# A hybrid decoder block on one core: zero matmuls before the first transposes, scale's first piece summed by TensorE, and pool means taken before the shift is added

## The chip, the cores and the metric

The kernel runs on one core of a Trainium2 chip. The metric is the device time of one execution in microseconds (us). The kernel before has a median of 923.67 us over 3 runs (922.73 to 924.28).

## The reference

One decoder block over 1024 tokens of width 1024, in float32. Two RMS norms with adaLN stand ahead of a mixer and an MLP. What matters here is the mixer's first part:

```
mod = silu(c) @ w_ada + b_ada                  # shift1, scale1, gate1, shift2, scale2, gate2
h = rms_norm(x, norm1_pre) * (1 + scale1) + shift1
z = h @ w_in                                   # 512 columns u, 512 columns v, 512 columns for the pool
v = layer_norm(gelu(v)); y_a = gelu(u) * (w_causal[head] @ v + b_spatial)      # chunks of 128 tokens
diff = mean over the last w tokens of z_b - z_b      # w = 2, 4, 8, 16 by group; at the start over the tokens there are
y_b = (diff @ w_pool[group] + b_pool) * pool_scale
mix = concat(y_a, y_b) @ w_out
```

The shift enters z as a constant row, shift1 @ w_in, the same for each token. A mean over a window less the token does not change when the same constant is added to all tokens.

## The kernel before, in words

The 1024 tokens are worked in two halves of 512. Features lie on the 128 partitions in eight blocks k, tokens along the free dimension. Every large product is made of three float32r matmuls (high by high, high by low, low by high); the high part of an operand is a ScalarE cast, the low part a VectorE subtraction.

`start()` (line 1339) is the first half's way from x to the mixer's outputs. Its instructions stand in the order written, on VectorE, ScalarE, TensorE, GpSimd and SyncE alike (`manual_schedule`, line 1664). What follows, `project()` among it, is ordered by the planner: it takes what is ready by its own costs, and may put such instructions between those of `start()`. In `start()`:

1. *Norm and transposes.* `first(i)` squares token tile i on ScalarE and has GpSimd take the power, `second(i)` scales the tile on VectorE, `third(i)` transposes three feature blocks on TensorE. `vectors_a()` transposes the loaded vectors.
2. *Scale in pieces.* `piece()` loads columns of w_ada, `piece_sum()` (line 1306) weighs eight tiles with silu(c) on VectorE into two accumulators and adds them (`both`), `piece_end()` (line 1322) sums over partitions by a matmul with ones, and `ada_vector()` (line 183) makes scale or shift of it. PIECES (line 1289) are 128, 128, 256, 256 and 256 columns.
3. *Pool.* `scaled_hi`, `scaled_lo` write a block's scaled tokens, and `pool_pass(k, n)` (line 1417) multiplies them with the pool columns of w_in, into four PSUM banks `pbs`. The shift is not in it yet.
4. *Values.* A loop over four pairs of blocks (line 1552) makes v with `value_step`, and beside it the shift's pieces. `row_sum` (line 1522) builds shift @ w_in for the three parts on VectorE, in `vacc`, `bacc` and `uacc`, and `row_vector` (line 1528) sums it over partitions on TensorE.
5. *Gates.* `gate_pass(k)` (line 1591) makes u; `values()` (line 442) is the layer norm of v. Then `row_vector(bacc)` gives the pool's shift, four ScalarE activations add it to the four zb tiles (line 1634), and `windowed(h, j, zb)` (line 379) keeps the last 16 tokens for the second half (halo), widens the window in one to four steps, corrects the first tokens and subtracts. `pool_out` multiplies with w_pool, `spatial_products` and `spatial_end` make the gated part.
6. *Output.* `stream.fill(n)` (line 28) makes sure that n tiles of w_out are loaded, cast and subtracted; `load_x(1)` loads the second half's tokens, into the buffers in which the pool columns of w_in lay (`braw`, line 1348); `normalise(1)` scales them. `project(0)` (line 554) multiplies with w_out, pool outputs first (MIX_ORDER), in two output halves, with the transposes of the second tokens between.

Buffers: tag `raw` has four, which hold one shift accumulator, the four u pairs `uraw` and then the w_out tiles; tags `whi`, `wlo` have four each, tag `acc` four, PSUM eight banks. The program prints the code:

Of the kernel before, what the change touches and what calls it, by code (L numbers as in the profile page):

```python
# [8 lines left out]
F32 = mybir.dt.float32  # L9
# [7 lines left out]
P = 128  # L17
# [23 lines left out]
def block_kernel(  # L41
# [78 lines left out]
    make_identity(nc, ident)  # L120
    ones = const.tile([P, P], F32, name="ones")
# [1184 lines left out]
    def piece_sum(blk, c0, n, ts):  # L1306
# [9 lines left out]
        def both():  # L1316
            a, b = [acc_of[blk][o][:, c0:c0 + n] for o in range(2)]
            nc.vector.tensor_tensor(a, a, b, ALU.add)

        return [step(kt) for kt in range(KT)] + [both]  # L1320

    def piece_end(blk, c0, n, split=False):
        pa = ps_tile(f"pa{blk}_{c0}")
        nk = n // P
        for k in range(nk):
            at = c0 + k * P
            nc.tensor.matmul(pa[:, k:k + 1], lhsT=acc_of[blk][0][:, at:at + P], rhs=ones[:, 0:1], start=True, stop=True)
        rest = lambda: ada_vector(blk, pa[:, 0:nk], range(c0 // P, c0 // P + nk))
        return rest if split else rest()
# [9 lines left out]
    def start():  # L1339
# [44 lines left out]
        def second(i):  # L1384
            nc.vector.tensor_scalar(xs[i], xs[i], rs[i], None, ALU.mult)
# [5 lines left out]
        g = piece_sum(1, *PIECES[0], sc[0])  # L1391
        first(0)
        first(1)
        vectors_a()
        second(0)
# [3 lines left out]
        third(1)  # L1399
        first(3)  # L1400
        second(2)
        third(2)
        weave(g)
        second(3)
        scale_rest = piece_end(1, *PIECES[0], split=True)
        third(3)
        scale_rest()
# [7 lines left out]
        pbs = [ps_tile(f"pb0_{j}") for j in range(NG)]  # L1415
# [23 lines left out]
        pool_pass(0, 0)  # L1439
        pool_pass(0, 1)  # L1440
        piece_end(1, *PIECES[1])
# [64 lines left out]
        value_lo(0, 1)  # L1506
        pool_pass(KT - 1, 1)
# [12 lines left out]
        bacc, vacc, uacc = rows_of("b"), rows_of("v"), accp.tile([P, 512], F32, tag="junk", bufs=1, name="shift_wu")  # L1520
# [31 lines left out]
        for kp in range(NQ):  # L1552
            if kp == 0:
                sh.append(piece(0, 2 * QC, QC))
                value_tiles(1)
                value_hi(1)
# [25 lines left out]
            if kp == 1:  # L1582
                rest_b()
                turn()
            if kp == 2:
                offsets()

# [28 lines left out]
        weave(sums_b(0, 4), sums_u(0, 2))  # L1616
        gate_load(3)
        gate_pass(2)
        gate_pass(3)
        steps, vs = values(0, pvs)  # L1620
        weave(steps[:4], sums_b(4, 8))
# [4 lines left out]
        weave(steps[4:], sums_u(2, 6))  # L1626
        gate_hi(3)
        gate_lo(3, 0)
        gate_lo(3, 1)
        gate_pass(5)  # L1630
        bvec = row_vector(bacc, "b")
        for j in range(NG):
            z = zbs[j][:, HALO:]
            nc.scalar.activation(z, z, AF.Identity, bias=bvec[:, j:j + 1])
        weave(sums_u(6, 8), windowed(0, 0, zbs[0]))
        gate_pass(6)
        gate_pass(7)
        psp = [spatial_products(0, j, vs) for j in range(2)]
        uvec = row_vector(uacc, "u")
        us = [gate(0, j, pus[j], uvec[:, j:j + 1]) for j in range(NHEAD)]  # L1640
        weave(windowed(0, 1, zbs[1]), windowed(0, 2, zbs[2]))
        psp += [spatial_products(0, j, vs) for j in range(2, NHEAD)]
        yb = [pool_out(0, j, pair_of(diffs[0], j)) for j in range(2)]
        weave(windowed(0, 3, zbs[3]))
# [3 lines left out]
        yb += [pool_out(0, j, pair_of(diffs[0], j)) for j in range(2, NG)]  # L1648
        load_x(1)
        measure, apply = normalise(1, "a")  # L1650
        ya = []
        for j in range(NHEAD):
            if j in (1, 2):
                stream.fill(1 + j)
            ya.append(spatial_end(0, j, psp[j], us[j]))
            if j < 2:
                yb[2 + j][1]()
            if j == 2:
                measure()
# [50 lines left out]
```

## Time and profile before

| | |
|---|---|
| median of 3 runs | 923.67 us (922.73 to 924.28) |
| the profiled execution | 922.04 us |
| its span, first to last instruction | 920.3 us |
| TensorE busy (matmul) | 889.4 us, 97% of the span |
| VectorE busy | 687.4 us, 75% |
| ScalarE busy | 419.1 us, 46% |
| GpSimd busy | 89.1 us, 10% |
| chain that ended last, by engine | TensorE 53%, issue 32%, VectorE 8%, ScalarE 4%, DMA 2% |

Busy time is a union over instructions of an engine; matmuls are pipelined, so that a row of x8 matmuls shows the time from the first start to the last end. A timeline row has the start, the time, the engine, the source line and what was written and read; a bracket behind it gives the idle time before, and what ended it. One fp32 matmul has two records.

### The profile page before, as it was taken

Reading aid. Unit: us, or ns where it says so; the run is one execution under the profiler, and the core shown is the slowest. Engines: PE = TensorE matmul, PEld = TensorE weight load, DVE = VectorE, ACT = ScalarE, POOL = GpSimd, SP = SyncE. Lnnn points to the kernel's source line nnn. Section 1 sums busy time; section 2 is a strip of 40 time slices with the busy share of each in tenths; the row PEclk is TensorE's granted clock in tenths of the full one; section 3 lists DMA queues with packets and bytes.
Section 4 is the critical chain, followed back from the end, with each engine's and each line's share of the span. In section 5 each row is a group of like instructions: output and inputs, shape, how many; then the busy total and the mean of one; then the engine's idle time right before and its main releaser. Section 6 shows DMA issues by size and latency. Waiting matters only on the chain.

```text
span 920.3 us, 10782 instructions
## 1 busy us (share of the span) xinstructions
PE 889.4 (97%) x3960; PEld 722.9 (79%) x3960; DVE 687.4 (75%) x980; ACT 419.1 (46%) x558; POOL 89.1 (10%) x147
## 2 busy tenths in 40 slices
PE   5999999999999989999999999999999999999995
PEld 3788678888887768888888888778888888888883
DVE  6989888799759896766666657567887774569796
ACT  3323674334367474444444354544455433434331
POOL 4001020013003001111100101100000000000032
PEclk9999999999999999999999999999999999999998
DMA  9934256575734148543444434499975884334664
GB/s 316 357 113 143 91 161 188 178 252 183 234 87 149 54 129 274 185 138 130 168 150 158 139 136 155 160 320 389 338 242 198 294 279 117 109 110 145 207 212 154
DMA packets 114105, 173.52 MB, mean 189 GB/s; under 512 B 6098, under 2 KB 61442, under 8 KB 114052
## 3 DMA queue, kind: packets, MB, share of 16 engines
q1 hardware_dynamic: 104292, 135.03, 45.8%
q0 software_dynamic: 9760, 37.80, 10.8%
q8 instruction: 31, 0.51, 0.2%
q14 instruction: 22, 0.18, 0.1%
HBM read 135.06 MB, written 37.75 MB: 188 GB/s over the span
## 4 chain that ended last, share of the span: by engine, by line
PE 53%; issue 32%; DVE 8%; ACT 4%; DMA 2%; POOL 1%; SPq 0%; POOLq 0%; DVEq 0%; ACTq 0%
PE a L828 6%; PE a L829 6%; PE a L830 6%; PE p L830 3%; PE p L829 3%; PE p L828 3%; PE pb L1421 3%; PE po L85 2%; PE pu L1596 2%; PE po L86 2%; PE po L87 2%; PE pv L85 2%; PE pv L87 2%; PE pv L86 2%; PE b L828 1%
## 5 line engine op out<-in xcount | busy, mean ns | idle before, releaser
L85 PE MATMUL m<-thi,shi 128*128 128x512 f32 x448 | 174.3, 389 | 0.0
L86 PE MATMUL m<-tlo,shi 128*128 128x512 f32 x448 | 174.3, 389 | 0.0
L87 PE MATMUL m<-thi,slo 128*128 128x512 f32 x448 | 174.3, 389 | 0.0
L94 DVE TENSOR_TENSOR slo<-s,shi 128x1024 fp32r<-128x1024 f32 x56 | 68.4, 1222 | 55.8 <-ACT shi L91 55.8
L91 ACT CAST shi<-s 128x1024 fp32r<-128x1024 f32 x56 | 58.9, 1052 | 106.2 <-PE m L86 64.1
L86 PEld LDWEIGHTS m<-tlo,shi 128*128 128x128 f32 x448 | 84.1, 188 | 17.6
L87 PEld LDWEIGHTS m<-thi,slo 128*128 128x128 f32 x448 | 84.1, 188 | 17.5
L85 PEld LDWEIGHTS m<-thi,shi 128*128 128x128 f32 x448 | 84.1, 188 | 17.3
L91 ACT CAST thi<-wt 128x1024 fp32r<-128x1024 f32 x40 | 42.1, 1052 | 39.7 <-DVE wt L571 31.3
L91 ACT CAST whi<-w_raw 128x1024 fp32r<-128x1024 f32 x28 | 29.3, 1053 | 52.0 <-DMA w_raw<-in_w_in_dram 15.4
L571 DVE TENSOR_TENSOR wt<-wt,b 128x1024 f32<-128x1024 f32 x32 | 39.1, 1222 | 15.0 <-DMA b<-in_w_fc_dram 13.1
L94 DVE TENSOR_TENSOR tlo<-wt,thi 128x1024 fp32r<-128x1024 f32 x40 | 48.9, 1223 | 1.4
L571 DVE TENSOR_TENSOR S<-c,F 128x1024 f32<-128x1024 f32 x12 | 14.7, 1224 | 41.8 <-ACT F L860 41.8
L94 DVE TENSOR_TENSOR wlo<-w_raw,whi 128x1024 fp32r<-128x1024 f32 x28 | 34.1, 1220 | 7.0 <-ACT whi L91 7.0
L858 ACT COPY F<-a 128x512 f32<-128x512 f32 x16 | 9.4, 586 | 57.0 <-PE a L830 57.0
L291 POOL TENSOR_TENSOR f<-msf,neg_half 128x1 f32<-128x1 f32 x8 | 7.2, 901 | 282.5 <-DVE msf L1160 282.5
L603 DVE TENSOR_TENSOR lob<-wa,hib 128x1024 fp32r<-128x1024 f32 x16 | 19.6, 1225 | 16.4 <-ACT hib L598 16.4
L598 ACT CAST hic<-wo 128x1024 fp32r<-128x1024 f32 x16 | 16.8, 1051 | 31.3 <-DVE wo L571 31.3
L598 ACT CAST hib<-wa 128x1024 fp32r<-128x1024 f32 x16 | 16.8, 1050 | 30.3 <-DVE wa L571 30.3
L181 DVE SCALAR_TENSOR_TENSOR ada_acc<-ada_raw,silu_c,ada_acc 128x1024 f32<-128x1024 f32 x21 | 26.9, 1280 | 3.9 <-DMA ada_raw<-in_w_ada_dram 3.8
L85 PE MATMUL po<-whi,ybs 128*128 128x512 f32 x64 | 25.8, 406 | 1.6 <-ACT yb L419 0.9
L830 PE MATMUL p<-hS,loc 128*128 128x512 f32 x64 | 25.4, 397 | 1.9 <-DVE loc L603 1.9
(311 smaller groups left out, 2194.4 us busy)
## 6 DMA issues: line engine op xcount, KB each, us to landing
s<-fD SPq DMA_DIRECT2D x56, 512.0 KB, 4.1
wt<-in_w_fc_dram SPq DMA_DIRECT2D x40, 512.0 KB, 5.1
ada_raw<-in_w_ada_dram SPq DMA_DIRECT2D x24, 512.0 KB, 4.8
fD<-S POOLq DMA_DIRECT2D x16, 768.0 KB, 3.7
wa<-in_w_fc_dram SPq DMA_DIRECT2D x20, 512.0 KB, 4.2
piece<-in_w_ada_dram SPq DMA_DIRECT2D x16, 512.0 KB, 8.3
w_raw<-in_w_out_dram SPq DMA_DIRECT2D x16, 512.0 KB, 4.6
wo<-in_w_fc_dram SPq DMA_DIRECT2D x16, 512.0 KB, 4.6
```

Of the source, the lines that this page charges most:

```text
L85: nc.tensor.matmul(ps, lhsT=ah, rhs=bh, start=start, stop=False)
L86: nc.tensor.matmul(ps, lhsT=ah, rhs=bl, start=False, stop=False)
L87: nc.tensor.matmul(ps, lhsT=al, rhs=bh, start=False, stop=stop)
L91: nc.scalar.copy(hi, src)
L94: nc.vector.tensor_tensor(lo, src, hi.bitcast(F32), ALU.subtract)
L181: nc.vector.scalar_tensor_tensor(acc, t, silu_c[:, kt:kt + 1], acc, ALU.mult, ALU.add)
L571: nc.vector.tensor_tensor(o, a, b, op)
L598: nc.scalar.copy(unit_tiles(kind, n)[0], src)
L828: nc.tensor.matmul(ps, lhsT=ah, rhs=bh, start=first, stop=False, skip_group_check=not start)
L829: nc.tensor.matmul(ps, lhsT=ah, rhs=bl, start=False, stop=False, skip_group_check=not start)
L830: nc.tensor.matmul(ps, lhsT=al, rhs=bh, start=False, stop=last, skip_group_check=not start)
L1421: nc.tensor.matmul(pbs[j], lhsT=w[:, j * P:(j + 1) * P], rhs=a, start=k == 0 and n == 0, stop=k == KT - 1 and n == 2)
```

## The change

- A tile `idle` of zeros is made, and `busy(n)` issues n matmuls of 512 bf16 columns from it into `pbs[0]`: 12 first of all, 5 behind the vectors' transpose, 2 behind the second tile's transposes, 2 behind the fourth's. The four `pbs` banks are taken earlier for that.
- Scale's first piece goes through `piece_direct`: eight matmuls with the loaded w_ada tiles as weights and silu(c) as the one column, into one PSUM column, in place of nine VectorE instructions and one matmul.
- For the other pieces `both` is gone: `piece_end` adds the two accumulators in PSUM, with two matmuls for each block of 128 columns. The second piece's end is moved one pool pass ahead.
- The second value weights are cast before the last two pool passes.
- The zb tiles stay without the shift. `windowed` of group 0 comes after the second round of the value loop, of group 1 after the third, of group 2 among the gates, of group 3 after the seventh gate pass; the pool outputs follow among the gate passes. The b row sums and the b vector come last, and four small VectorE instructions add the b vector to the halo.
- The u row sums start later, the first two ahead of `stream.fill(1)`, the other six after the last gate pass. `load_x(1)` stands behind the b sums, and `measure` and `apply` behind all spatial ends.

```diff
--- before.py
+++ after.py
@@ -118,6 +118,8 @@
     nc.gpsimd.dma_start(out=rows_a[V_BA:NVA, :], in_=b_ada.rearrange("(r q) -> r q", q=P))
     ident = const.tile([P, P], F32, name="ident")
     make_identity(nc, ident)
+    idle = tmp.tile([P, 512], BF16, tag="t", name="idle")
+    nc.vector.memset(idle, 0.0)
     ones = const.tile([P, P], F32, name="ones")
     nc.vector.memset(ones, 1.0)
     neg_half = const.tile([P, 8], F32, name="neg_half")
@@ -1313,20 +1315,23 @@
                 else:
                     nc.vector.scalar_tensor_tensor(acc, ts[kt], silu_c[:, kt:kt + 1], acc, ALU.mult, ALU.add)
             return run
-        def both():
-            a, b = [acc_of[blk][o][:, c0:c0 + n] for o in range(2)]
-            nc.vector.tensor_tensor(a, a, b, ALU.add)
-
-        return [step(kt) for kt in range(KT)] + [both]
-
-    def piece_end(blk, c0, n, split=False):
+        return [step(kt) for kt in range(KT)]
+
+    def piece_end(blk, c0, n):
         pa = ps_tile(f"pa{blk}_{c0}")
         nk = n // P
         for k in range(nk):
             at = c0 + k * P
-            nc.tensor.matmul(pa[:, k:k + 1], lhsT=acc_of[blk][0][:, at:at + P], rhs=ones[:, 0:1], start=True, stop=True)
-        rest = lambda: ada_vector(blk, pa[:, 0:nk], range(c0 // P, c0 // P + nk))
-        return rest if split else rest()
+            for o in range(2):
+                nc.tensor.matmul(pa[:, k:k + 1], lhsT=acc_of[blk][o][:, at:at + P], rhs=ones[:, 0:1], start=o == 0, stop=o == 1)
+        ada_vector(blk, pa[:, 0:nk], range(c0 // P, c0 // P + nk))
+
+    def piece_direct(blk, c0, ts):
+
+        pa = ps_tile(f"pa{blk}_{c0}")
+        for kt in range(KT):
+            nc.tensor.matmul(pa[:, 0:1], lhsT=ts[kt], rhs=silu_c[:, kt:kt + 1], start=kt == 0, stop=kt == KT - 1)
+        return lambda: ada_vector(blk, pa[:, 0:1], range(c0 // P, c0 // P + 1))
 
     def scaled_hi(ps, k):
         a = hact.tile([P, 2, HT], F32R, tag="h", name=f"ha0_{k}")
@@ -1388,22 +1393,31 @@
             for k in range(3):
                 nc.tensor.transpose(out=pts[k][:, i * P:(i + 1) * P], in_=xs[i][:, k * P:(k + 1) * P], identity=ident)
 
-        g = piece_sum(1, *PIECES[0], sc[0])
+        pbs = [ps_tile(f"pb0_{j}") for j in range(NG)]
+
+        def busy(n):
+
+            for _ in range(n):
+                nc.tensor.matmul(pbs[0], lhsT=idle[:, 0:P], rhs=idle, start=True, stop=True)
+
+        busy(12)
         first(0)
         first(1)
         vectors_a()
+        busy(5)
         second(0)
         third(0)
         first(2)
         second(1)
         third(1)
+        busy(2)
         first(3)
         second(2)
         third(2)
-        weave(g)
+        scale_rest = piece_direct(1, 0, sc[0])
         second(3)
-        scale_rest = piece_end(1, *PIECES[0], split=True)
         third(3)
+        busy(2)
         scale_rest()
         for i in range(NT):
             nc.gpsimd.tensor_tensor(rinv[0][:, i:i + 1], pws[i], half[:, 0:1], ALU.pow)
@@ -1412,7 +1426,6 @@
 
 
         hT = []
-        pbs = [ps_tile(f"pb0_{j}") for j in range(NG)]
 
         def pool_pass(k, n):
             w = (whi, whi, wlo)[n][k // 2][:, k % 2]
@@ -1437,8 +1450,8 @@
         weave(g[KT // 2:])
         pool_lo(0)
         pool_pass(0, 0)
+        piece_end(1, *PIECES[1])
         pool_pass(0, 1)
-        piece_end(1, *PIECES[1])
         his(1)
         pool_pass(0, 2)
         more(3)
@@ -1504,6 +1517,8 @@
         value_hi(0)
         value_lo(0, 0)
         value_lo(0, 1)
+        value_tiles(1)
+        value_hi(1)
         pool_pass(KT - 1, 1)
         pool_pass(KT - 1, 2)
         zbs = []
@@ -1517,7 +1532,7 @@
         def rows_of(n):
             return fact.tile([P, 512], F32, tag="f", name=f"shift_w{n}")
 
-        bacc, vacc, uacc = rows_of("b"), rows_of("v"), accp.tile([P, 512], F32, tag="junk", bufs=1, name="shift_wu")
+        vacc, uacc = rows_of("v"), accp.tile([P, 512], F32, tag="junk", bufs=1, name="shift_wu")
 
         def row_sum(acc, k, src):
             if k == 0:
@@ -1552,8 +1567,6 @@
         for kp in range(NQ):
             if kp == 0:
                 sh.append(piece(0, 2 * QC, QC))
-                value_tiles(1)
-                value_hi(1)
                 gate_load(0)
             elif kp < NQ - 1:
                 value_tiles(kp + 1)
@@ -1582,8 +1595,10 @@
             if kp == 1:
                 rest_b()
                 turn()
+                weave(windowed(0, 0, zbs[0]))
             if kp == 2:
                 offsets()
+                weave(windowed(0, 1, zbs[1]))
 
 
         pus = [ps_tile(f"pu0_{j}") for j in range(NHEAD)]
@@ -1613,50 +1628,53 @@
         for i in range(NT):
             nc.tensor.matmul(pvs[i], lhsT=ones_r, rhs=vb[:, 0], start=False, stop=False)
             nc.tensor.matmul(pvs[i], lhsT=ones_r, rhs=vb[:, 1], start=False, stop=True)
-        weave(sums_b(0, 4), sums_u(0, 2))
         gate_load(3)
+        weave(windowed(0, 2, zbs[2]))
         gate_pass(2)
         gate_pass(3)
         steps, vs = values(0, pvs)
-        weave(steps[:4], sums_b(4, 8))
+        weave(steps[:4])
         gate_hi(2)
         gate_lo(2, 0)
         gate_lo(2, 1)
         gate_pass(4)
-        weave(steps[4:], sums_u(2, 6))
+        weave(steps[4:])
         gate_hi(3)
         gate_lo(3, 0)
         gate_lo(3, 1)
+        yb = [pool_out(0, j, pair_of(diffs[0], j)) for j in range(2)]
         gate_pass(5)
-        bvec = row_vector(bacc, "b")
-        for j in range(NG):
-            z = zbs[j][:, HALO:]
-            nc.scalar.activation(z, z, AF.Identity, bias=bvec[:, j:j + 1])
-        weave(sums_u(6, 8), windowed(0, 0, zbs[0]))
-        gate_pass(6)
-        gate_pass(7)
-        psp = [spatial_products(0, j, vs) for j in range(2)]
-        uvec = row_vector(uacc, "u")
-        us = [gate(0, j, pus[j], uvec[:, j:j + 1]) for j in range(NHEAD)]
-        weave(windowed(0, 1, zbs[1]), windowed(0, 2, zbs[2]))
-        psp += [spatial_products(0, j, vs) for j in range(2, NHEAD)]
-        yb = [pool_out(0, j, pair_of(diffs[0], j)) for j in range(2)]
-        weave(windowed(0, 3, zbs[3]))
+        weave(sums_u(0, 2))
         for y, low in yb:
             low()
         stream.fill(1)
-        yb += [pool_out(0, j, pair_of(diffs[0], j)) for j in range(2, NG)]
-        load_x(1)
-        measure, apply = normalise(1, "a")
+        gate_pass(6)
+        weave(windowed(0, 3, zbs[3]))
+        yb += [pool_out(0, 2, pair_of(diffs[0], 2))]
+        gate_pass(7)
+        weave(sums_u(2, 8))
+        psp = [spatial_products(0, j, vs) for j in range(2)]
+        uvec = row_vector(uacc, "u")
+        yb += [pool_out(0, 3, pair_of(diffs[0], 3))]
+        us = [gate(0, j, pus[j], uvec[:, j:j + 1]) for j in range(NHEAD)]
+        psp += [spatial_products(0, j, vs) for j in range(2, NHEAD)]
+        yb[2][1]()
+        yb[3][1]()
+        stream.fill(2)
+        bacc = accp.tile([P, 512], F32, tag="acc", name="shift_wb")
+        rest_u = sums_b(0, KT)
         ya = []
         for j in range(NHEAD):
-            if j in (1, 2):
-                stream.fill(1 + j)
             ya.append(spatial_end(0, j, psp[j], us[j]))
-            if j < 2:
-                yb[2 + j][1]()
-            if j == 2:
-                measure()
+            if j == 1:
+                stream.fill(3)
+            weave(rest_u[4 * j:4 * j + 4])
+        load_x(1)
+        bvec = row_vector(bacc, "b")
+        for j in range(NG):
+            nc.vector.tensor_scalar(halo[:, j, :], halo[:, j, :], bvec[:, j:j + 1], None, ALU.add)
+        measure, apply = normalise(1, "a")
+        measure()
         apply()
         return ya + [y for y, low in yb]
 
```

## Rows read from the trace of the kernel before

**Rows 1.** Windows view: PE, PEld, DVE, ACT, POOL busy; clock; DMA; GB/s.

```profile
25.00:30.00 5.00, 5.00 (x27) 4.10 (x27) 4.96 (x12) 2.21 (x4) 0.00 (x0) 1.00 1.08 368
```

**Rows 2.** What TensorE waited for between 135 us and the end, longest in total.

```profile
PE p L830 <- DVE loc L603: 1.9, 1, 1.9
```

**Rows 3.** TensorE's timeline to 24 us: start, us, instructions, [idle before <-releaser].

```profile
8.81 1.88 PE L1389 MATMUL pta<-ident,x 128*128 128x128 f32 x6 [1.83 <-DVE x L1385]
...
15.36 3.78 PE L1421 MATMUL pb<-ha,wbhi 128*128 128x512 f32 x8 [0.35 <-ACT ha L1333]
...
21.25 1.18 PE L1421 MATMUL pb<-ha,wbhi 128*128 128x512 f32 x4
...
23.82 0.61 PE L1327 MATMUL pa<-ones,ada_acc 128*128 128x1 f32 x4 [1.39 <-DVE ada_acc L1318]
```

**Rows 4.** ScalarE's timeline, first 24 us.

```profile
13.22 0.62 ACT L1368 CAST wbhi<-x 128x512 fp32r<-128x512 f32 x1 [2.80 <-DMA x<-in_w_in_dram]
```

**Rows 5.** VectorE's timeline, first 24 us.

```profile
16.01 1.13 DVE L1314 SCALAR_TENSOR_TENSOR ada_acc<-piece,silu_c,ada_acc 128x128 f32<-128x128 f32 x4
...
19.67 0.61 DVE L1312 TENSOR_SCALAR ada_acc<-piece,silu_c 128x256 f32<-128x256 f32 x2
...
23.34 0.42 DVE L1318 TENSOR_TENSOR ada_acc<-ada_acc,ada_acc 128x256 f32<-128x256 f32 x1
```

**Rows 6.** TensorE's timeline, 97 to 130 us.

```profile
97.86 0.95 PE L1531 MATMUL pau<-ones,shift_wu 128*128 128x1 f32 x8
...
98.67 2.03 PE L468 MATMUL psp<-wcT,vs 128*128 128x128 f32 x16
...
100.53 2.74 PE L417 MATMUL pp<-diff,wpl 128*128 128x512 f32 x6
...
107.42 0.50 PE L85 MATMUL po<-whi,ybs 128*128 128x512 f32 x1 [0.88 <-ACT yb L419]
...
129.61 3.65 PE L324 MATMUL pta<-ident,x 128*128 128x128 f32 x32
```

**Rows 7.** VectorE's timeline, 48 to 104 us.

```profile
48.54 0.69 DVE L1468 TENSOR_TENSOR wvwlo<-vraw,wvwhi 128x512 fp32r<-128x512 f32 x1 [2.47 <-ACT wvwhi L1465]
...
69.47 1.53 DVE L1526 SCALAR_TENSOR_TENSOR shift_wv<-vraw,shift,shift_wv 128x512 f32<-128x512 f32 x2
...
74.45 0.48 DVE L1524 TENSOR_SCALAR shift_wb<-x,shift 128x512 f32<-128x512 f32 x1
...
90.57 1.29 DVE L1549 TENSOR_TENSOR wuwlo<-uraw,wuwhi 128x512 fp32r<-128x512 f32 x2
...
99.55 0.17 DVE L384 COPY halo<-zb 128x16 f32<-128x16 f32 x1
...
102.77 0.69 DVE L399 SCALAR_TENSOR_TENSOR diff<-s,zb 128x512 f32<-128x512 f32 x1
```

**Rows 8.** SyncE's queue: the first load of w_out, in its timeline.

```profile
76.72 0.38 SPq L242 DMA_DIRECT2D w_raw<-in_w_out_dram  x1
```

**Rows 9.** What SyncE's queue waited for, 60 to 130 us.

```profile
SPq L242 <- DVE shift_wu L1526: 17.0, 4, 9.3
```

**Rows 10.** Loaded w_out tiles, 70 to 131 us: casts, subtractions, landing.

```profile
L91 ACT CAST whi<-w_raw x7: 1035/1045/1054, 104.3 to 124.3; 128x1024 fp32r<-128x1024 f32 x7
...
L94 DVE TENSOR_TENSOR wlo<-w_raw,whi x7: 1211/1219/1226, 105.3 to 125.9; 128x1024 fp32r<-128x1024 f32 x7
...
DMA to landing us min/median/max: 3.8/4.6/4.7
```

**Rows 11.** ScalarE's timeline: the four gates of the first tokens.

```profile
99.04 2.42 ACT L458 ACTIVATE u<-pu,vecu 128x512 f32<-128x512 f32 x4
```

**Rows 12.** VectorE's timeline, 106 to 128 us.

```profile
106.47 0.75 DVE L473 SCALAR_TENSOR_TENSOR ya<-psp,vec,Bsp 128x512 f32<-128x512 f32 x1
...
127.06 0.68 DVE L94 TENSOR_TENSOR yas<-ya,yas 128x512 fp32r<-128x512 f32 x1
```

**Rows 13.** VectorE by line, 117 to 127 us: after the second tokens' squares.

```profile
L296 DVE TENSOR_SCALAR msa<-ssa 128x1 f32<-128x1 f32 x4 | 0.6, 152 | 2.4 <-ACT junka L308 2.4
```

## The prediction

> **What bounds the kernel now.** I read the windows first. TensorE fills its stretches: between 25 and 30 us it is busy 5.00 of 5.00 us [rows 1], and so are the stretches up to 100 us. The list of waits from 135 us to the end has six entries for TensorE, the longest 1.9 us [rows 2]. So whatever time is lost or won before the last matmul of the first tokens' first output half, at 129.6 us, is carried to the end nearly unchanged, and the working can stop there.
>
> Then I read the timelines for the stretches in which TensorE does not set the pace itself. There are two. The first is the start: the first eight pool matmuls come at 15.36 us and take 3.78 us, 0.45 us each, while four at 21.25 us take 1.18 us, under 0.3 us each [rows 3]. That is the lower of the clock's two levels (1.2 GHz) and then the upper (2.4 GHz); the granted-clock column reads 1.00 all the while, so here only the spacing shows it. Before the rise TensorE had worked without a real gap from 15.36 us on; the transposes from 8.81 us, six in 1.88 us, had not raised it. The 1.39 us gap ahead of 23.82 us did not lower it again [rows 3]. The second stretch is 98 to 130 us, where the last gates, the pool outputs and the first w_out matmuls wait on VectorE and ScalarE.
>
> **The start.** Scale's first piece no longer costs VectorE its nine instructions ahead of the fourth tile's scaling, but that gain is cut off: the first pool weights land only in time for a cast at 13.22 us, which takes 0.62 us [rows 4], and the first scaled tile follows it on ScalarE (0.69 us), so the first pool pass cannot start before 14.5 us. I take that, instead of 15.36. The twelve zero matmuls stand where TensorE waits for DMA anyway, so they cost nothing while that cover lasts; the eight direct products (16 records) fit into the wait for the fourth tile if the clock is up.
> From 14.5 us: the second piece's four later steps took 1.16 us at 16.01 us [rows 5]; behind the low half (0.66 us) they now end at about 16.4, so TensorE's moved piece end starts there, the scale is made by 17.4 us, and the third piece's sums start then and not at 19.67 us [rows 5]. They run 3.67 us to 21.1; the adding at 23.34 us (0.42 us) is gone [rows 5]. The piece's matmuls, now eight records, end at 22.0, where TensorE left them at 24.3. **Gain 2.3 us.**
>
> **The price of leaving out the adding.** Each 128-column block now needs two matmuls, four records for two. Eight such records take the time from 97.86 to 98.67 us, 0.10 us each [rows 6]. After the third piece twelve blocks remain, 24 records more, 2.4 us, all of them where TensorE is full [rows 1]. The VectorE work saved there was not on the path. **Loss 2.4 us**; the first gate pass begins as before, at 71.5 us, within 0.3.
>
> **The value stage.** The second weight cast is moved up, which takes VectorE's wait of 2.47 us at 48.54 us away [rows 7]; four addings (0.4 us each) go as well, 4.1 us in all. The windowed means of the first two groups take their place: the fourth group's six steps last from 99.55 to 103.4 us, 3.8 us [rows 7], and each group before it has one step (0.7 us) less, so 1.7 and 2.4 us. VectorE comes out even. The third shift piece now waits for an older buffer and is issued some 5 us later; I count nothing, since its sums come more than 10 us after that.
>
> **From the gates to the output.** VectorE's list from 74.45 us to the last gate subtraction (from 90.57 us, 1.29 us) is 17.3 us long without a gap [rows 7]. Fourteen row sums leave it (0.66 to 0.77 us each, the dependent pair at 69.47 us takes 1.53 us [rows 7]): 9.6 us. The third group's means, 3.1 us, come in, and about 0.7 us of waiting for the norm's power. So it ends at 86.0, and the first two u rows at 87.3.
> Here the change puts a wait on VectorE. The first w_out tile is loaded into the buffer that these two u rows release: before, it was issued at 76.72 us [rows 8], and the queue's waits name the u sums as releaser [rows 9]. It had 27 us until its use. Now its subtraction stands right behind: landing 4.6 us, cast 1.05 us, subtraction 1.22 us [rows 10] end at 94.2, and queued behind are the fourth group's means (3.8 us, to 98.0) and the other six u rows (6 times 0.77 us, to 102.6). With the handovers I take 103.0.
> TensorE would start the u vector at 97.86 us less 0.8 (the b vector's matmuls are gone from there) plus three pool outputs of 0.92 us (six records at 100.53 us, 2.74 us [rows 6]), so at 99.8. **It waits 3.2 us.** From 103.0: u vector 0.8, last pool output 0.9, two spatial products 1.86 (98.67 to 100.53 us [rows 6]) make 106.6. The gates, 2.42 us for four [rows 11], now stand behind that pool output's two activations and give their PSUM buffers from 106.8 on, so the w_out matmuls start then. Before, they ran unbroken from 107.42 us with three done already [rows 6], which is the same as 106.7. **So far nothing is won or lost.**
> After the gates comes the second w_out tile's cast and subtraction, and the first spatial end starts at 110.9, not 106.47 us [rows 12]. From there to the last yas subtraction, 127.7 us [rows 12], VectorE had 21.3 us. Out of it go two pool subtractions and one w_out subtraction, 2.3 us, and the squares' stretch, 0.6 us busy and 2.4 us waiting [rows 13]; in come eight b rows, 5.5 us. That leaves 21.5 us, so it ends at 132.4, **4.7 us later**. TensorE's first half ended 1.9 us behind it (the transposes follow at 129.61 us [rows 6]).
> Unknown is the order that the planner gives to the later w_out tiles. Before, seven subtractions lie between 105.3 and 125.9 us [rows 10], ahead of the last yas; if three of them (3.4 us) go behind it, the loss is 1.3 us. If the loads of the second tokens, which now wait for the b sums, end last instead, I bound the loss at 7 us (landing 4.6 us, four squares, scaling). The b vector's 0.8 us falls into a wait. I take 4.5, nearest to the order that the rows show.
>
> **Sum.** -2.3 + 2.4 + 0 + 0 + 4.5 less rounding: +4.5 us. The profiled execution has 922.04 us, a span of 920.3 and 1.7 around it; 926.5 would be its successor. The median of the runs is 923.67, 1.6 above it, so I say **928.2 us**. Own range of this case: 925.0 to 930.7. A measurement of this kernel can tell about 0.2% (1.85 us) from no change.
>
> **Rivals.**
> 1. *Faster: the first w_out tile is in time.* If its buffer comes free earlier, or VectorE reaches the u rows later than I count, the wait before 94.2 vanishes: it is worth 4.3 us (94.2 less the subtraction, less 87.3 and the two pool subtractions of 0.6). The u vector then starts at 99.8, w_out at 103.5 and not 106.7, and if TensorE's order hides the b sums, 3.2 us less 0.8 for the b vector stay: -2.4, 921.3 us. It decides once VectorE idles under 1 us ahead of that subtraction. Against it: [rows 9]. Chance 0.2.
> 2. *No change: TensorE goes around the late yas.* The 72 matmuls of the second half that don't need the last pair could fill the wait, if PSUM buffers are free. Then only the 1.3 us stay, or less: 924.5 us. Chance 0.2.
> 3. *The clock is down at the pool passes.* The zeros, or what follows them, don't hold the level. Then 16 slow records (0.26 us, from 12.0 to 16.2) and three slow transposes put the first pass at 18.0, and it runs at 0.45: 3.6 us more, 931.8 us. The gap of 1.39 us that left the clock up speaks against it [rows 3], as no gap here is longer. Chance 0.06.
> The Trainium skill, "TensorE: Matmul & The Clock Gate", Part 4, says that a transpose does not count as work for the clock. Six slow transposes ahead of 15.36 us agree [rows 3]; by that rule only the few zero matmuls hold the clock from 9 to 14 us, which is this rival.
>
> **How the numbers follow.** My forecast has 0.54. Slower by over 0.2%: forecast and third rival, 0.60. Same: 0.20. Faster: 0.20. The range from 921.3 to 931.0 leaves out half of the first rival and most of the third.
>
> **What would show it.** Pool matmuls 0.24 us apart from the first one, at 14.5 us; the third piece's matmuls at 21 us; TensorE busy from there to 99 us; VectorE idle for some 4 us before the first w_out subtraction; the u vector at 103 us; the last yas subtraction near 132 us. Wrong would be a u vector before 100.5 us, or a yas end before 129 us.

## The result, and the profile after

The changed kernel takes 946.74 us (945.28 to 946.94, 4 runs), the one before 923.69 us beside it: a ratio of 1.0247, with a 95% interval of 1.0229 to 1.0265. It is 23.05 us slower. The prediction said 928.2 us and slower: the side is right, but the forecast loss of 4.5 us is a fifth of the measured one, and the time lies far outside the range of 925.0 to 930.7. The profiled execution has 946.9 us, its span 945.2 us.

First, what TensorE waited for up to 160 us in the changed kernel (engine, line, releaser; us in total, times, longest):

```profile
PE pab L1546 <- DVE shift_wb L1541: 17.1, 1, 17.1
PE pau L1546 <- DVE shift_wu L1541: 3.5, 1, 3.5
PE pta L1394 <- DVE x L1390: 1.6, 3, 0.7
```

One wait of 17.1 us, at the four matmuls (eight records) of the b vector, is new. The wait for the u vector, 3.5 us, is the one that was forecast at 3.2. From 135 us to the end the list of TensorE's waits has the same six entries as before, each within 0.1 us, the longest 1.9 us as in [rows 2]; so the loss was made ahead of there.

TensorE's timeline of the changed kernel around that wait:

```profile
99.64 1.95 PE L470 MATMUL psp<-wcT,vs 128*128 128x128 f32 x16
105.05 1.83 PE L1546 MATMUL pau<-ones,shift_wu 128*128 128x1 f32 x8 [3.47 <-DVE shift_wu L1541]
106.75 2.05 PE L419 MATMUL pp<-diff,wpl 128*128 128x512 f32 x2
108.59 3.09 PE L470 MATMUL psp<-wcT,vs 128*128 128x128 f32 x16
128.78 1.84 PE L1546 MATMUL pab<-ones,shift_wb 128*128 128x1 f32 x8 [17.10 <-DVE shift_wb L1541]
130.48 0.77 PE L85 MATMUL po<-whi,ybs 128*128 128x512 f32 x1
131.05 0.63 PE L86 MATMUL po<-wlo,ybs 128*128 128x512 f32 x1
...
134.47 0.58 PE L85 MATMUL po<-whi,ybs 128*128 128x512 f32 x1
134.89 0.39 PE L86 MATMUL po<-wlo,ybs 128*128 128x512 f32 x1
```

The first w_out matmul (`po`) stands right behind the b vector, at 130.48 us; before, three were done ahead of 107.42 us [rows 6]. The transposes of the second tokens, at 129.61 us before [rows 6], begin at 154.95 us. So the whole first output half was moved by 25 us; it was not made longer (24.5 us from its first matmul to the transposes, against 24.3). The two profiled executions are 24.9 us apart.

What VectorE did meanwhile, from its timeline in the changed kernel:

```profile
95.24 1.22 DVE L94 TENSOR_TENSOR wlo<-w_raw,whi 128x1024 fp32r<-128x1024 f32 x1 [1.75 <-ACT whi L91]
...
100.22 4.68 DVE L1541 SCALAR_TENSOR_TENSOR shift_wu<-uraw,shift,shift_wu 128x512 f32<-128x512 f32 x6
104.82 0.68 DVE L424 TENSOR_TENSOR ybs<-yb,ybs 128x512 fp32r<-128x512 f32 x1
110.30 0.69 DVE L424 TENSOR_TENSOR ybs<-yb,ybs 128x512 fp32r<-128x512 f32 x1 [4.79 <-ACT ybs L423]
113.55 1.23 DVE L94 TENSOR_TENSOR wlo<-w_raw,whi 128x1024 fp32r<-128x1024 f32 x1 [2.56 <-ACT whi L91]
114.69 0.74 DVE L475 SCALAR_TENSOR_TENSOR ya<-psp,vec,Bsp 128x512 f32<-128x512 f32 x1
...
126.31 2.32 DVE L1541 SCALAR_TENSOR_TENSOR shift_wb<-x,shift,shift_wb 128x512 f32<-128x512 f32 x3
...
133.53 0.69 DVE L94 TENSOR_TENSOR yas<-ya,yas 128x512 fp32r<-128x512 f32 x1 [0.68 <-ACT yas L91]
```

The last b row ends at 128.6 us, behind two spatial ends and three w_out subtractions. The last yas subtraction (`yas` holds the gated outputs, `ybs` the pool's) ends at 134.22 us, 1.8 us behind the forecast of 132.4. That this end was nearly met is partly luck: the first spatial end comes at 114.69 us and not at 110.9, while three w_out subtractions that were counted into the list (3.4 us) fell behind it. What TensorE does beside the list was not foreseen. VectorE also stands idle for 4.79 and 2.56 us just ahead of that list.

Windows of the changed kernel (busy time and number of instructions of PE, PEld, DVE, ACT, POOL; then TensorE's granted clock, DMA share, GB/s):

```profile
15.00:20.00 5.00, 4.89 (x15) 3.52 (x14) 4.72 (x15) 1.19 (x2) 1.41 (x3) 0.54 1.09 356
20.00:25.00 5.00, 5.00 (x25) 4.24 (x24) 3.02 (x11) 0.76 (x2) 0.00 (x0) 0.78 1.09 359
...
105.00:110.00 5.00, 4.95 (x17) 3.95 (x18) 0.50 (x1) 1.29 (x3) 0.00 (x0) 0.50 0.63 211
...
120.00:125.00 5.00, 0.00 (x0) 0.00 (x0) 4.03 (x6) 2.51 (x3) 0.00 (x0) 0.50 0.61 198
125.00:130.00 5.00, 1.22 (x6) 1.25 (x7) 4.89 (x7) 0.00 (x0) 0.00 (x0) 0.50 0.65 182
130.00:135.00 5.00, 5.00 (x14) 4.04 (x15) 3.38 (x10) 2.71 (x6) 0.02 (x1) 0.51 0.68 239
```

The granted clock was at its lower level (0.50 of full speed, 1.2 GHz) in two stretches: in the pool passes behind the zeros, and in and after the waits of the late stretch. The ten w_out matmuls from 130.48 us took 4.4 us; at the 0.235 us of those from 134.89 us on it would be 2.35.

### The profile page after: what moved, and what is told of

The parts are those of the page before. It is cut to its first block, busy times and chain, and to the rows that moved or that the text cites. A ratio compares the mean times of both kernels' runs of the same rounds, so it can differ in the third digit from the quotient of the medians.

```text
span 945.2 us, 10898 instructions
## 1 busy us (share of the span) xinstructions
PE 903.7 (96%) x4024; PEld 734.6 (78%) x4025; DVE 685.4 (73%) x968; ACT 417.5 (44%) x554; POOL 87.0 (9%) x147
## 4 chain that ended last, share of the span: by engine, by line
PE 53%; issue 31%; DVE 9%; ACT 3%; DMA 1%; POOL 1%; SPq 0%; POOLq 0%; DVEq 0%; ACTq 0%
PE a L830 5%; PE a L832 5%; PE a L831 5%; PE po L85 3%; PE po L87 3%; PE po L86 3%; PE p L832 3%; PE pb L1434 3%; PE p L831 3%; PE p L830 3%; PE pv L85 2%; PE pv L87 2%; PE pv L86 2%; PE b L830 1%; PE b L831 1%
## 5 line engine op out<-in xcount | busy, mean ns | idle before, releaser
L573 DVE TENSOR_TENSOR wt<-wt,b 128x1024 f32<-128x1024 f32 x32 | 39.1, 1222 | 17.7 <-DMA b<-in_w_fc_dram 14.3
```

What stands on the lines that cost most here:

```text
L573: nc.vector.tensor_tensor(o, a, b, op)
```

## The experiments

Diffs are against the changed kernel unless said otherwise; the kernel before measured 923.69 to 923.99 us beside all of them. A ratio is to the kernel before, with its 95% interval.

**Which half of the change.** The start alone (zeros, direct piece, accumulators not added, second piece's end moved) on the kernel before:

> The kernel before with the start's part of the change alone (zeros, direct first piece, piece ends without the adding). By the changed kernel's trace the first gate pass begins 2.0 us later than before: 925.7 us, with the clock down between 15 and 22 us. If the adding's price and the clock's fall are not what makes these 2 us, the time is that of before, 923.7, or better by the 2.3 us forecast.

924.31 us, ratio 1.0003 (0.9994 to 1.0013). And the rest alone (second value weights, means, sums and loads), with the start as before:

> The kernel before with the pool means' part alone, b vector last. Order theory: TensorE waits for the b sums as in the changed kernel, 20 to 23 us slower than before: 944 to 947 us. If the clock at the start were a cause of the long wait, it would be under 940 us.

947.19 us, ratio 1.0251 (1.0234 to 1.0268), with TensorE's waits as in the full change:

```profile
PE pab L1533 <- DVE shift_wb L1528: 17.6, 1, 17.6
PE pau L1533 <- DVE shift_wu L1528: 4.9, 1, 4.9
```

The whole loss comes from the second half of the change. The value stage adds nothing to it: the first pool pass comes at 16.27 us and the first gate pass at 72.36, both 0.9 us later than before. Dropping only the zeros (all `busy(n)` calls) from the full change:

> The changed kernel without the zero matmuls. If they hold the clock up where it pays, the sixteen direct records and the first pool passes run at the lower level and it is 2 to 4 us slower: 949 to 951 us. If their clock is lost again before the pool passes, it is within 1.5 us of the changed kernel: 945 to 948 us.

948.31 us, ratio 1.026 (1.0244 to 1.0275): between the two expectations. The median is 1.6 us above the changed kernel's, but the ranges of the two (945.28 to 946.94 and 946.59 to 949.35) overlap, and so do the intervals, so what the zeros give here is not settled.

**The place of the b vector on TensorE.** The vector and its halo additions go out of `start()` into the stretch where the planner places work, so that the vector stands behind 72 of the 96 w_out matmuls of the first output half; its accumulator moves to another buffer for that (the edit is shortened):

```diff
-        bacc = accp.tile([P, 512], F32, tag="acc", name="shift_wb")
+        bacc = rows_of("b")
...
-        bvec = row_vector(bacc, "b")
-        for j in range(NG):
-            nc.vector.tensor_scalar(halo[:, j, :], halo[:, j, :], bvec[:, j:j + 1], None, ALU.add)
...
     def prepare(key, h, n, name):
         def run():
+            pool_shift()
```

> Order theory: in the changed kernel the b vector's eight records stand on TensorE ahead of the first w_out matmul and wait 17.1 us for the b row sums; emitted between the two output halves they let the w_out matmuls start when the gates give their banks, near 111.5 us and not at 130.5, and the first half then ends about 2 us behind the last yas subtraction (133.5 us in the changed kernel): 946.7 less some 19 us, 926 to 929 us. Rival, VectorE's list ends the stretch whatever TensorE's order: no more than 4 us are won, 942 us or more.

939.22 us, ratio 1.0156 (1.014 to 1.0172): 7.5 us of the 23. Neither theory had this. TensorE's waits from 95 to 160 us in this kernel:

```profile
PE pau L1546 <- DVE shift_wu L1541: 3.2, 1, 3.2
PE pta L326 <- DVE x L319: 2.7, 1, 2.7
PE po L85 <- ACT yas L91: 2.0, 1, 2.0
PE pab L1546 <- DVE shift_wb L1541: 1.1, 1, 1.1
```

The 17 us wait is gone, but the transposes come at 143.91 us, still 14.3 later than before [rows 6]. Two rows of VectorE's timeline in this kernel tell why:

```profile
137.50 0.75 DVE L181 TENSOR_SCALAR ada_acc<-ada_raw,silu_c 128x1024 f32<-128x1024 f32 x1 [2.65 <-DMA ada_raw<-in_w_ada_dram]
138.17 0.69 DVE L94 TENSOR_TENSOR yas<-ya,yas 128x512 fp32r<-128x512 f32 x1
```

The planner puts five w_out subtractions (122.41 to 131.4 us, 1.22 us each) around the last four b rows, where the changed kernel had two in this stretch, and ahead of the last yas one operation that waits 2.65 us for its load. So the last yas falls to 138.17 us, and the second tokens' x, whose loads wait for the b rows, is 2.7 us late at the transposes. So the b rows' place on VectorE seems to cost twice, by the vector and by what stands behind the rows; the run that moves the rows, below, tests this.

**How long the wait is.** Two of the eight b rows, one behind each of the first two spatial ends:

```diff
-        rest_u = sums_b(0, KT)
+        rest_u = sums_b(0, 2)
...
-            weave(rest_u[4 * j:4 * j + 4])
+            weave(rest_u[j:j + 1])
```

> Of the eight b row sums only the first two are left (the pool's shift vector is made of a quarter of the rows), one behind each of the first two spatial ends; the b vector stands where it stood. The six rows left out are 4.6 us of VectorE. Theory (TensorE stands at the b vector until the last b row): the b vector comes at 121 to 123 us in place of 128.78, its wait falls from 17.1 to about 10 us, first w_out matmul near 123 to 125; time 940 to 942. Rival (the wait is only the visible place, the last yas subtraction binds anyway): the time falls by the rows' own 4.6 us or less, 942 to 946.

940.05 us, ratio 1.0178 (1.0153 to 1.0204); the wait fell to 10.8 us:

```profile
122.67 1.83 PE L1546 MATMUL pab<-ones,shift_wb 128*128 128x1 f32 x8 [10.82 <-DVE shift_wb L1541]
```

The b vector came 6.1 us earlier: 4.6 us of rows, 1.2 us of a w_out subtraction that the planner now puts behind the second row, and 0.4 us that this execution was ahead by already. TensorE stood until the last b row, however early or late that was.

**The place of the b rows on VectorE.** All eight go ahead of the last pool output's subtraction, into the 4.79 us of idle time seen above; the b vector stays where it was on TensorE:

```diff
+        bacc = accp.tile([P, 512], F32, tag="acc", name="shift_wb")
+        weave(sums_b(0, KT))
         yb[3][1]()
...
-            weave(rest_u[4 * j:4 * j + 4])
```

> The changed kernel with its eight b row sums moved up on VectorE, from between the spatial ends to ahead of the last pool output's subtraction, where VectorE idled 4.79 and 2.56 us (105.5 to 113.55 us) in the changed kernel; the b vector stays where it stood on TensorE, ahead of the first w_out matmul. Theory (TensorE stands at the b vector because VectorE makes it behind the first two spatial ends; the second tokens' loads wait for the same rows): rows end near 111.5 us, the b vector's wait falls from 17.1 us to under 2, first w_out matmul at 112 to 114 us, the last yas near 128 us, time 926 to 931. Rival (the b rows' VectorE time anywhere in this stretch makes the loss): 938 or more.

931.18 us, ratio 1.008 (1.0063 to 1.0096): 15.6 us of the 23, and 0.2 us above the range expected. TensorE's waits from 95 to 160 us, and the b vector in its timeline:

```profile
PE pau L1546 <- DVE shift_wu L1541: 3.3, 1, 3.3
PE pta L326 <- DVE x L319: 1.3, 1, 1.3
112.02 1.02 PE L1546 MATMUL pab<-ones,shift_wb 128*128 128x1 f32 x8
```

The same eight rows, the same vector, the same TensorE order, and no wait for it: two thirds of the loss were where VectorE ran the rows. They took 5.9 us from 105.88 us on; the subtraction behind them came at 111.79 us (110.30 in the changed kernel), the w_out subtraction after it at 114.02 (113.55).

**The u rows.** Back to their old places among the gates:

```diff
+        weave(sums_u(0, 2))
         gate_load(3)
...
-        weave(steps[4:])
+        weave(steps[4:], sums_u(2, 6))
...
-        weave(sums_u(0, 2))
+        weave(sums_u(6, 8))
         for y, low in yb:
...
-        weave(sums_u(2, 8))
```

> The eight u row sums go back to their old places among the gates, all else as in the changed kernel; the first w_out tile can be loaded early again. In the changed kernel VectorE idled 1.25, 0.70 and 1.75 us around that tile's subtraction at 95.24 us and ran six u rows (4.68 us) after it, so the u vector came at 105.05 us. Theory of the serial list (VectorE's late list, b rows last, holds TensorE at the b vector): everything from the u vector on comes 4 to 7 us earlier, the b vector near 122 to 125 us, time 940 to 943, and the b vector still ends TensorE's longest wait, at 15 us or more. Rival (the b vector's place alone matters, the u vector's wait is swallowed): 945.5 to 947.

941.45 us, ratio 1.0192 (1.0177 to 1.0207): 5.3 us less than the changed kernel. The u vector came without a wait, 5.0 us earlier, and the b vector behind a wait as long as ever:

```profile
100.09 0.95 PE L1546 MATMUL pau<-ones,shift_wu 128*128 128x1 f32 x8
121.98 1.84 PE L1546 MATMUL pab<-ones,shift_wb 128*128 128x1 f32 x8 [17.95 <-DVE shift_wb L1541]
```

In this execution 1.3 of the 5.0 us lie ahead of the gates (first gate pass at 72.00 us, 73.32 in the changed kernel), where the edit changes nothing and the clock at the start differs. With the b vector's late place as well:

> Both repairs together: u row sums at their old places, and the b vector behind the first w_out matmuls. Alone they measured 941.45 and 939.22, 5.3 and 7.5 us below the changed kernel. Theory (two separate causes, and a third left: the b rows between the spatial ends delay the last yas and the second tokens' loads): the gains add, 932 to 936, with TensorE's first wait behind the w_out matmuls at the transposes or the late yas. Rival A (both act on the same wait): 937 to 940. Rival B (no third cause): 924 to 927.

932.33 us, ratio 1.0097 (1.0079 to 1.0114): the gains add (7.5 and 5.3 from 946.74 leave 933.9), and 8.5 us over before remain, as the theory of a third cause had it. With the b rows in the idle time instead:

> The u row sums at their old places and the b rows in VectorE's idle time ahead of the last pool output's subtraction, all else as changed; alone the two edits measured 941.45 (5.3 us under the changed kernel) and 931.18 (15.6 under). Theory (their gains add, and what is then left over the kernel before is the added matmuls' 2.2 us less the start's gain and what the means give): 924 to 927.5, no TensorE wait over 2 us ahead of the w_out matmuls. Rival (a third cause in this stretch, not yet seen): 928.5 to 931.

923.49 us, ratio 1.0001 (0.9991 to 1.0011), half a microsecond under the range expected. TensorE's longest wait from 95 to 160 us:

```profile
PE pab L1546 <- DVE shift_wb L1541: 1.0, 1, 1.0
```

These two moves, 15.6 us and then 7.7, take back the whole loss; none is left for a further cause in this stretch.

**The two matmuls per block.** The start alone on the kernel before, with the accumulators of the later pieces added on VectorE as before (the edit is against the start alone, and `piece_end` has one matmul for each block again):

```diff
+        def both():
+            a, b = [acc_of[blk][o][:, c0:c0 + n] for o in range(2)]
+            nc.vector.tensor_tensor(a, a, b, ALU.add)
+
-        return [step(kt) for kt in range(KT)]
+        return [step(kt) for kt in range(KT)] + [both]
```

> The kernel before with the change's start (zero matmuls, first piece summed by TensorE), but the two accumulators of the later pieces still added on VectorE, so that TensorE has no added matmuls. The start with the added matmuls alone measured 924.31 (ratio 1.0003). Prediction's theory (24 added records cost 2.4 us where TensorE is full, and the start gains 2.3): 921.5 to 922.3. Rival (the added matmuls are hidden in gaps, or the start's gain is lost otherwise): 923.5 to 924.5.

922.10 us, ratio 0.9985 (0.9974 to 0.9996), against 924.31 with the added matmuls. The pool pass behind the third piece's matmuls, and the first gate pass, from TensorE's timeline with the added matmuls and then without:

```profile
21.66 1.17 PE L1434 MATMUL pb<-ha,wbhi 128*128 128x512 f32 x4
...
71.17 1.98 PE L1609 MATMUL pu<-ha,wuwhi 128*128 128x512 f32 x8
```

```profile
22.26 1.18 PE L1437 MATMUL pb<-ha,wbhi 128*128 128x512 f32 x4
...
69.14 1.98 PE L1612 MATMUL pu<-ha,wuwhi 128*128 128x512 f32 x8
```

The first gate pass comes 2.0 us earlier without them. The two executions are not alike at the start, though: the granted clock was 1.00 throughout in the first, and 0.50 from about 13.8 to 16.5 us in the second. From the upper to the lower row it is 49.5 us with the added matmuls and 46.9 without (47.2 in the kernel before, from 24.29 to 71.47 us): 2.3 to 2.6 us for the 24 records, 2.4 forecast. The gain of the start is 24.29 less 21.66, 2.6 us with the clock up; 71.47 less 69.14, 2.3 us, is what it left after that fall of the clock. The same edit on the kernel with both sums moved:

> As the last one, with the accumulators of the later pieces added on VectorE again. Theory (the added matmuls' price, 922.1 against 924.31 with the means unmoved, is the same here): 2.2 us under the last one, 922 to 925. Rival (with the means in VectorE's value stage, the three addings of 0.4 us each come into a wait): within 1 us of the last one.

923.38 us, ratio 0.9991 (0.998 to 1.0003): here no gain can be told. The first gate pass comes 1.4 us earlier (71.59 against 73.00), but the b vector's wait grows from 1.0 to 2.9 us, for VectorE's last row ends no earlier (the vector is at 106.50 us against 106.09), and the clock falls behind it:

```profile
105.00:110.00 5.00, 3.50 (x12) 3.20 (x13) 4.41 (x6) 1.75 (x3) 0.00 (x0) 0.56 0.88 298
```

The second tokens' transposes so end 1.5 us later. That the profiled executions still take the same time goes with a fall of the clock in the other one, at 0.50 from about 344 to 348 us; how the ten runs of each come out alike is not settled.

**The clock in the waits.** 20 idle matmuls ahead of the u vector and 135 ahead of the b vector:

> The changed kernel with TensorE kept busy while it waits: 20 matmuls of 256 bf16 columns ahead of the u vector and 135 ahead of the b vector, overwritten afterwards. In the changed kernel the granted clock was 0.50 from about 104.5 us and from 114.5 to 134.8 us; the b vector took 1.70 us against 0.82 and the first ten w_out matmuls 4.4 us against 2.3, and the last pool output's matmul came some 1.9 us later for it. Theory (the fallen clock is a loss of its own on top of the waits): 3 to 5 us less, 941.5 to 944. Rival (the clock's loss is hidden by the waits of VectorE and ScalarE): 945.5 to 947.

943.24 us, ratio 1.0213 (1.02 to 1.0226), 3.5 us less. The clock was up from 100 to 125 us. From the u vector to the first of the four gates it is 3.4 us here (102.85 to 106.24 us) and 5.1 us in the changed kernel (105.05 to 110.17 us), so the fallen clock cost 1.7 us there. The rest of the 3.5 us is not shown to be the clock in the waits: the first gate pass came 1.6 us earlier (71.74 us against 73.32), the planner also put six w_out matmuls (121.63 to 123.3 us) ahead of the b vector, and behind the last 1.5 us wait the clock was down all the same (0.66 from 125 to 130 us).

**Towards a better kernel.** All row sums, loads and the norm as before, the means moved up and without the shift:

> The means stay moved up and without the shift, the start as changed; but all row sums, b and u, the loads of x and w_out and the norm stand where they stood before, and the b vector (for the halo alone) behind the sixth gate pass. Theory (the loss is the b and u sums' new place): no b wait, u vector at 96 to 99 us, first w_out matmul at 101 to 105 against 105.4 before, transposes of the second tokens between 125 and 130 us; time 919 to 924. Rival (the moved means themselves cost, on VectorE in the value stage or in buffers): 926 or more.

925.83 us, ratio 1.0029 (1.0016 to 1.0041), between the theory's 924 and the rival's 926, and nearer to the rival. TensorE waited once, in the gates:

```profile
PE pu L1611 <- DVE wuwlo L1564: 2.3, 1, 2.3
```

The third group's means (3.1 us) stand ahead of a gate subtraction that TensorE is waiting for. With those means behind the last gate subtraction, and the accumulators added on VectorE (the edit against the last kernel, without the accumulators' part):

```diff
         gate_load(3)
-        weave(windowed(0, 2, zbs[2]))
...
-        weave(sums_u(6, 8))
+        weave(sums_u(6, 8), windowed(0, 2, zbs[2]))
```

> Means moved up and without the shift for groups 0 and 1, group 2's behind the last gate subtraction and group 3's where the change has it; row sums, loads and norm as before, the b vector for the halo alone; the changed start, but the two accumulators added on VectorE. Theory (taken out of the stretch from 92 to 103 us, the first two groups' means and four ScalarE additions free TensorE's gaps of 0.33, 0.65 and 0.88 us ahead of the w_out matmuls): 1.0 to 2.5 us under the 922.1 of the same start with the means unmoved: 919.5 to 921.2. Rival (the gaps are set by the w_out tile's cast and the pool outputs' activations, which stay): 922 to 923.5.

921.14 us (11 runs), ratio 0.9974 (0.9964 to 0.9985): 0.3% faster than the kernel before, and the gaps of 0.33, 0.65 and 0.88 us ahead of the w_out matmuls are gone; a wait of 1.0 us is left in the gates. Its interval overlaps that of the start alone with the accumulators added on VectorE (0.9974 to 0.9996), so what the means add to the start's gain is not settled.

## Why the prediction was wrong

- **The failed step is one sentence: "The b vector's 0.8 us falls into a wait."** It priced the vector by its length, and not by what stands behind it on TensorE. Inside `start()` the instructions keep the order written, and the first w_out matmul came out behind the vector. So TensorE did not work through w_out from 106.8 us on while VectorE went down its list: it stood for 17.1 us until the last b row, and w_out began at 130.48 us. The code shows the vector at the end of `start()` and the w_out matmuls in `project()` after it. The planner may put w_out matmuls ahead of the vector (in the run with idle matmuls it put six there), but here it put none, and no run shows why. The prediction looked at who waits on VectorE and on SyncE's queue; "TensorE's order" stands only as a condition of its first rival, and the sum never asked which TensorE instruction is next in line behind the new wait. Its signs of being wrong, a u vector before 100.5 us or a yas end before 129 us, didn't look at the first w_out matmul either, and neither came.
- **The term for the list, +4.7 us, was too small even without that wait.** With the b vector behind 72 matmuls the kernel is still 11 us above the forecast (939.22 against 928.2). The bounds given for the two unknowns, 1.3 us to 7 us, did not hold what both did together, and the two ranges of the prediction (925.0 to 930.7 and, further down, 921.3 to 931.0) are both far too low: in that kernel w_out subtractions went between the b rows, and the second tokens' loads waited for the same rows.
- **The late w_out tile** was right: buffer freed by the u rows, VectorE idle for 1.25, 0.70 and 1.75 us around its subtraction, u vector at 105.05 us (2.05 us behind the forecast 103.0, of which 1.85 us came from a later first gate pass), wait 3.5 us (3.2). But "so far nothing is won or lost" was not. The first gate ended at about 110.8 us (the four take 2.41 us from 110.17 us on) and not at 106.8: to the 2.05 us the clock, at 0.50 after that wait, added 1.7 us, as the run with idle matmuls shows. The prediction put the clock behind the wait at nothing. And old places for the u rows give 5.3 us (7.7 with the b rows in the idle time), since VectorE's whole list behind them starts that much earlier.
- **The start** was right by its terms: in the start alone the gain by the third piece was 2.6 us (2.3 forecast), the added matmuls took 2.3 to 2.6 us (2.4), and the first gate pass came at 71.17 us, 0.3 us from 71.5 as said, with the clock up all the way. In the changed kernel it came at 73.32 us, 2.2 us later. That is the third rival, given 0.06, in part: the granted clock fell to 0.50 at about 15.4 us, in the first pool pass. In the run with the late b vector the rival came as it was written: the clock fell before the sixteen direct records, the first pool pass came at 17.36 us (18.0 forecast) and the first gate pass at 74.28, 3.1 us later than in the start alone (3.6 forecast). The argument against that rival, that no gap is longer than the 1.39 us that had left the clock up, did not hold: in the changed kernel no gap from the zeros to that fall was over 0.8 us. By the Trainium skill, "TensorE: Matmul & The Clock Gate", Part 4, a transpose does not count as work for the clock in the way that other matmuls do; the start alone and the changed kernel neither prove nor break that, since the same instructions held the level in the one and lost it in the other.
- **The first rival** (tile in time, 0.2) fell with the idle time above, **the second** (TensorE goes around) with the order: it had nothing to go around with, for all 96 w_out matmuls of the first half stood behind the vector.
- **The value stage at nothing** held: no TensorE wait is left between 25 and 100 us.

## What to carry to other kernels

When a step is moved to "where it is not needed yet", find the next instruction behind its consumer on that consumer's engine: a matmul of 0.8 us whose operand comes late holds everything that comes after it in that engine's order, here 96 matmuls for 17 us. Then look where the engine that makes the operand stands idle: eight row sums, moved from between the spatial ends to a gap of 4.79 us a few instructions earlier, gave back 15.6 us, and the w_out subtraction behind the gap came 0.5 us later. An operand's reader may also hold a buffer that a load waits for (the u rows and the first w_out tile, the b rows and the second tokens), so moving the reader moves the load.

## What was not expected of the hardware

The level of TensorE's clock behind the zeros was not the same from one execution to the next with the same instructions ahead of it. The pool matmuls of the first pass began at 14.71 us in the start alone and at 14.68 in the changed kernel; the granted clock was 1.00 from 12 to 24 us in the start alone, 0.54 from 15 to 20 us in the changed kernel, and already 0.72 from 10 to 15 us in the one with the late b vector. It came back while TensorE worked on without a wait. One kernel's runs show it too: over ten executions of the start alone the three with a mean granted clock of 0.994 took 922.4 to 923.3 us, the five with 0.990 took 924.7 to 926.0.

In waits it fell as well: in the changed kernel TensorE was idle from 101.6 us, and the 5 us from 105 us on were at 0.50. But the length of a wait alone did not tell. In the kernel before, the gap of 1.39 us [rows 3] and the waits of 0.33, 0.65 and 0.88 us ahead of the w_out matmuls had not lowered it; in the start alone waits of 0.34, 0.64 and 0.88 us at the same place did. Windows from 105 to 110 us, in the kernel before and then in the start alone:

```profile
105.00:110.00 5.00, 3.76 (x14) 2.62 (x15) 3.97 (x7) 4.47 (x7) 0.00 (x0) 1.00 0.34 103
```

```profile
105.00:110.00 5.00, 4.06 (x11) 2.82 (x12) 4.19 (x6) 4.17 (x7) 0.00 (x0) 0.78 0.30 105
```

The w_out matmuls after the last of these waits began 0.3 us earlier in the start alone than before, and the second tokens' transposes 1.2 us later. So part of what a better start gains can be lost again in another stretch. The last kernel of the experiments had no such waits there; in its profiled execution the clock fell at 342 us (0.50 to 344 us), behind a wait of 1.94 us that the kernel before has as well, with the clock at 1.00 behind it.
